# A hybrid decoder layer on one core: where the token sums lie in SBUF, when attention's rows are loaded, and how far ahead gated rows are fetched

## The chip, the cores and the metric

The kernel runs on one core of a Trainium2 chip. The time is that of one execution on the device in microseconds, the median of three runs. The engines are TensorE (PE), VectorE (DVE), ScalarE (ACT), GpSimd (POOL) and SyncE (SP, which issues most DMAs); each runs its own instructions in the order in which they stand, and semaphores join them.

## The reference

One decoder layer on x (1, 512, 2048) in fp32: token mixing by two groups of heads in parallel, then a gated MLP with a short causal convolution.

```python
h = rmsnorm(x, attn_pre_norm)
proj = h @ w_in                       # gq, gk, gv, gg, ga, dq, dk, dv
log_a = log_sigmoid(ga @ w_alpha_up + b_alpha) / 16
o_a = gla_chunked(gq, gk, gv, log_a)  # 4 heads, dk 128, dv 256
o_a = rmsnorm(o_a, gla_norm) * silu(gg)
o_b = diff_attention(dq, dk, dv, lam) # 4 heads: softmax(q1 k1) - lam softmax(q2 k2), causal, ALiBi
o_b = rmsnorm(o_b, diff_norm) * (1 - lambda_init)
x = x + rmsnorm(concat(o_a, o_b) @ w_o, attn_post_norm)
h = rmsnorm(x, ffn_pre_norm)
a, b = split(h @ w_ffn_in)            # 2 x 5632
f = (gelu(causal_conv3(a)) * b) @ w_ffn_out
x = x + rmsnorm(f, ffn_post_norm)
```

## The kernel before

Every fp32 operand is split in two fp32r parts, hi (ScalarE, L125 or L138) and lo (VectorE, L126 or L139), and a product is three products on TensorE. Activations are held whole and transposed in `ah` and `al`. Weights stream in granules of 128x1024 (512 KB) through the tiles `raw` and `rt`, loaded by SP or, with an addition on the way, by POOL, and split into `whi` and `wlo`. A granule of `mm_n` (L182 to L184) is four groups of six 128x512 products.

Most projections run by Strassen's scheme, as a `Unit`: seven segments x0, z0, y0, z1, x1, y1, y2 with sums of activations (s5, s2, s3, s7) and sums of weights. The activation sums, here called token sums, are made once on VectorE by generators in the list `fill`; a call of `step()` draws as much from it as `pace[0]` says, and `drain()` draws the rest. The sums s5, s2 and s3 lie in the pool `so`.

The stages in order of time:

1. `first_half(0)` (0 to about 53 us on VectorE) loads x, normalizes it (L411), transposes it (L146) and multiplies the first four value granules. Its tiles lie in the pool `sa`, closed afterwards. The remaining value granules follow in `proj_n`, whose outputs `gvs` are stored to `gvd`. In between `fill` draws the token sums (`mixer_sums`, rows of `q`) and the forget gate's input (`forget_in`: `gas`, then 32 products, L556 and L557). Then come the eight units. The pool `mb` holds their outputs, the tiles of the setup (masks, `keep`, the lambdas, the columns `cols`), `gas`, `gvs` and the sums s7 (`s7r`); its tag `u` has four slots that all of these share.
2. From about 400 us the attention's steps are woven into the projections of the last head, of the gates (`proj_n` on C_GG) and of `w_o`. `tick()`, called after each group of six products, moves two chains by their paces (`GLA_PACE`, `DIFF_PACE`) and takes one entry from the list `turns`. A GLA head (`gla_head`, `gla_tail`) starts with the scores (L753), then decay rows (L727, L728), seven levels of products (L744) with masks (L747), a state and an output. Its inputs are DRAM rows that the units stored: `gr` (q, k, decay), `dr`, `dv`, `gv`. In `gla_rows(c)` the gated rows of two heads are fetched (`sg` from `sgd`, `ro` from `god`), multiplied (L962), transposed (L146) and split into `ah` and `al`.
3. `w_o`, the norms, and the feed-forward part, which starts with `first_pair(0)` and `first_pair(1)` by `proj_t` and then runs units with sums of its own, `up_sums` (L1198 to L1215).

Inside the manual schedules the order on TensorE is that of the code (in the first half and at the feed-forward start that of all engines); elsewhere a list scheduler sets the order on each engine, from the same code and from the buffers' release. A tile of a pool that lies on another pool's space waits for that space's last reader.

The lines in words that need showing are these two:

```python
gla_in = {0: gla_load(0)}      # after drain() and sums.close()
diff_load(0)
```

and the rows in `gla_rows`: `turns.extend(lambda t=t: run(t) for t in range(NT + 2))`, so that one tick fetches row t and transposes row t − 2.

## Time and profile before

| what | value |
|---|---|
| time, median of 3 runs | 2148.69 us (2147.42 to 2149.38) |
| the profiled execution's own time | 2146.62 us |
| its span | 2144.9 us |
| mean granted TensorE clock | 0.991 |
| PE, DVE, ACT, POOL busy | 97%, 72%, 45%, 12% |
| DMA traffic | 353.30 MB, mean 165 GB/s |

The span is what the profiler records, from the first to the last instruction; the rest of the execution's time lies around it. In rows of the timeline the columns are start, duration, engine, line, operation, output and inputs, how many in a row, and in brackets how long the engine was idle before and what released it. [...]

### The profile page before, as it was taken

Reading aid. Unit: us, or ns where it says so; the run is one execution under the profiler, and the core shown is the slowest. Engines: PE = TensorE matmul, PEld = TensorE weight load, DVE = VectorE, ACT = ScalarE, POOL = GpSimd, SP = SyncE. Lnnn points to the kernel's source line nnn. Section 1 sums busy time; section 2 is a strip of 40 time slices with the busy share of each in tenths; the row PEclk is TensorE's granted clock in tenths of the full one; section 3 lists DMA queues with packets and bytes.
Section 4 is the critical chain, followed back from the end, with each engine's and each line's share of the span. In section 5 each row is a group of like instructions: output and inputs, shape, how many; then the busy total and the mean of one; then the engine's idle time right before and its main releaser. Section 6 shows DMA issues by size and latency. Waiting matters only on the chain.

```text
span 2144.9 us, 34818 instructions
## 1 busy us (share of the span) xinstructions
PE 2081.1 (97%) x14161; PEld 1901.4 (89%) x14161; DVE 1553.2 (72%) x1873; ACT 960.9 (45%) x1217; POOL 260.1 (12%) x297
## 2 busy tenths in 40 slices
PE   7999999899999999989999999999999999999997
PEld 5899999788777888889999999999999887888886
DVE  7967667577764236487878787786777877988987
ACT  5445344344643234245444544554554554544433
POOL 2110111012110000001111111111111011110101
PEclk9999999999999999999999999999999999999999
DMA  7676775744345344346675776757667787676653
GB/s 260 149 178 156 165 178 120 257 139 143 114 137 206 96 138 167 128 99 148 142 190 141 172 173 149 175 140 191 149 161 191 223 215 187 170 196 174 175 159 137
DMA packets 253731, 353.30 MB, mean 165 GB/s; under 512 B 14128, under 2 KB 183524, under 8 KB 251780
## 3 DMA queue, kind: packets, MB, share of 16 engines
q1 hardware_dynamic: 181956, 266.14, 36.5%
q0 software_dynamic: 71616, 84.95, 24.8%
q8 instruction: 111, 1.82, 0.3%
q14 instruction: 48, 0.39, 0.1%
HBM read 303.33 MB, written 47.71 MB: 164 GB/s over the span
## 4 chain that ended last, share of the span: by engine, by line
PE 29%; issue 24%; DVE 3%; POOL 2%; DMA 2%; ACT 0%; POOLq 0%; DVEq 0%; ACTq 0%
PE bank L322 8%; PE bank L321 8%; PE bank L320 8%; PE bank L163 1%; PE bank L161 1%; PE bank L162 1%; DVE wlo L126 1%; POOL rt L234 1%; POOL raw L234 1%; DMA raw<-in_w_ffn_out_dram 1%; PE bank L1430 0%; PE bank L1431 0%; PE bank L1429 0%; DMA raw<-in_w_ffn_in_dram 0%; DVE u L1463 0%
## 5 line engine op out<-in xcount | busy, mean ns | idle before, releaser
L125 ACT ACTIVATE whi<-raw 128x1024 fp32r<-128x1024 f32 x314 | 331.7, 1060 | 554.6 <-PE bank L321 183.7
L126 DVE TENSOR_TENSOR wlo<-raw,whi 128x1024 fp32r<-128x1024 f32 x314 | 381.4, 1220 | 257.9 <-ACT whi L125 257.6
L125 ACT ACTIVATE whi<-rt 128x1024 fp32r<-128x1024 f32 x306 | 322.8, 1060 | 359.2 <-PE bank L321 200.6
L126 DVE TENSOR_TENSOR wlo<-rt,whi 128x1024 fp32r<-128x1024 f32 x306 | 373.2, 1221 | 141.1 <-ACT whi L125 140.5
L320 PE MATMUL bank<-ah,whi 128*128 128x256 f32 x1600 | 443.2, 277 | 3.9 <-ACT gvs L535 2.0
L322 PE MATMUL bank<-ah,wlo 128*128 128x256 f32 x1600 | 443.3, 277 | 2.3 <-DVE wlo L126 2.3
L321 PE MATMUL bank<-al,whi 128*128 128x256 f32 x1600 | 442.8, 277 | 0.0
L320 PEld LDWEIGHTS bank<-ah,whi 128*128 128x128 f32 x1600 | 301.4, 188 | 5.1 <-ACT gvs L535 2.5
L322 PEld LDWEIGHTS bank<-ah,wlo 128*128 128x128 f32 x1600 | 301.3, 188 | 2.9 <-DVE wlo L126 2.8
L321 PEld LDWEIGHTS bank<-al,whi 128*128 128x128 f32 x1600 | 301.2, 188 | 0.1
L1306 PE MATMUL bank<-wlo,ah 128*128 128x512 f32 x560 | 218.2, 390 | 1.3 <-DVE wlo L126 1.3
L1307 PE MATMUL bank<-whi,al 128*128 128x512 f32 x560 | 217.8, 389 | 0.0
L1305 PE MATMUL bank<-whi,ah 128*128 128x512 f32 x560 | 213.1, 390 | 4.5 <-DVE acc L1313 1.8
L182 PE MATMUL bank<-whi,ah 128*128 128x512 f32 x448 | 185.6, 416 | 0.1
L183 PE MATMUL bank<-wlo,ah 128*128 128x512 f32 x448 | 176.6, 395 | 0.4 <-DVE wlo L126 0.2
L184 PE MATMUL bank<-whi,al 128*128 128x512 f32 x448 | 176.4, 395 | 0.0
L1305 PEld LDWEIGHTS bank<-whi,ah 128*128 128x128 f32 x560 | 104.9, 188 | 28.8 <-ACT whi L125 3.9
L1306 PEld LDWEIGHTS bank<-wlo,ah 128*128 128x128 f32 x560 | 105.1, 188 | 23.9 <-DVE wlo L126 2.0
L1307 PEld LDWEIGHTS bank<-whi,al 128*128 128x128 f32 x560 | 105.1, 188 | 21.8
L322 PE MATMUL bank<-s2h,wlo 128*128 128x256 f32 x400 | 111.5, 279 | 1.9 <-DVE wlo L126 1.9
L320 PE MATMUL bank<-s3h,whi 128*128 128x256 f32 x400 | 110.8, 277 | 1.4 <-ACT s3h L138 1.4
L320 PE MATMUL bank<-s5h,whi 128*128 128x256 f32 x400 | 110.6, 277 | 1.0 <-ACT whi L125 1.0
(278 smaller groups left out, 4341.9 us busy)
## 6 DMA issues: line engine op xcount, KB each, us to landing
raw<-in_w_ffn_in_dram SPq DMA_DIRECT2D x96, 512.0 KB, 5.1
raw<-in_w_in_dram SPq DMA_DIRECT2D x64, 512.0 KB, 4.5
raw<-in_w_ffn_out_dram SPq DMA_DIRECT2D x48, 512.0 KB, 5.5
rt<-in_w_ffn_in_dram SPq DMA_DIRECT2D x40, 512.0 KB, 6.3
rt<-in_w_ffn_in_dram POOLq DMA_DIRECT2D x40, 512.0 KB, 5.9
raw<-in_w_ffn_in_dram POOLq DMA_DIRECT2D x40, 512.0 KB, 7.2
raw<-in_w_o_dram SPq DMA_DIRECT2D x32, 512.0 KB, 3.9
rt<-in_w_ffn_out_dram SPq DMA_DIRECT2D x20, 512.0 KB, 6.8
```

The source lines that it names most:

```text
L125: act(hi, raw, AF.Copy)
L126: tt(lo, raw, hi.bitcast(F32), ALU.subtract)
L182: mm(banks[t], ah[:, t, s, :], w[0][:, k, :], start=st, stop=False)
L183: mm(banks[t], ah[:, t, s, :], w[1][:, k, :], start=False, stop=False)
L184: mm(banks[t], al[:, t, s, :], w[0][:, k, :], start=False, stop=sp)
L234: nc.gpsimd.dma_start(out=raws[g].rearrange("p (a b) -> p a b", a=self.a), in_=self.block(0, j, g), accum_op=ALU.add)
L320: mm(o, wh, sh[:, :, kk, :], start=start and kk == 0 and n == 0, stop=False, **NOW)
L321: mm(o, wh, sl[:, :, kk, :], start=False, stop=False, **NOW)
L322: mm(o, wl, sh[:, :, kk, :], start=False, stop=kk == HK - 1, **NOW)
L1305: mm(b[j], sh[:, o:o + P], w[0][:, q, :], start=start and st == 0, stop=False, **NOW)
L1306: mm(b[j], sh[:, o:o + P], w[1][:, q, :], start=False, stop=False, **NOW)
L1307: mm(b[j], sl[:, o:o + P], w[0][:, q, :], start=False, stop=st == 3, **NOW)
```

## The change

It has these parts:

- The pool `so` of the token sums opens at the other end of SBUF (`side="right"`, with a pad tile), in a stack of its own, `early`. The pools `rq` and `mb`, which lay behind it, move down; they now lie on the space of `sa`, the first half's pool.
- `early` closes in the last unit, behind its z1, the last product with a token sum. In its place opens the pool `ga`, which takes the rows of the attention (`gr`, `dr`, `dv`, `gv`, `qb`) and the staging tiles `qs` and `sg`. The loads of the first GLA head and the first differential head are issued there, the other GLA heads' at the third step of the head before (n == 2).
- The unit's loads for x1 get a method of their own, `fetch21`, which the last unit calls ahead of the GLA rows.
- Gated rows: `gla_rows(0)` is called a granule earlier (i == 6), `gla_rows(1)` at i == 1 of `w_o`; a row is fetched at every second tick and so transposed four ticks after its fetch, not two.
- `GLA_PACE` goes from 1.45 to 1.5; the closing loop ends when `turns` is empty too.
- `proj_t` calls `step()` after each granule where it has no tick, which is so in `first_pair(1)` alone.

```diff
-GLA_PACE, DIFF_PACE = 1.45, 0.68
+GLA_PACE, DIFF_PACE = 1.5, 0.68
...
     def proj_t(w3, col, emit, order=tuple(range(KT // 4)), tick=None):
...
+            if tick is None:
+                step()
...
+        def fetch21(self):
+            self.b21 = [load(self.block(1, 0, g), self.a) for g in range(2)]
+
         def x1(self):
-            self.b21 = [load(self.block(1, 0, g), self.a) for g in range(2)]
+            if self.b21 is None:
+                self.fetch21()
...
-    so = sums.enter_context(tc.tile_pool(name="so", bufs=1, reuse_waits="tile"))
+    early = ExitStack()
+    so = early.enter_context(tc.tile_pool(name="so", bufs=1, side="right", reuse_waits="tile"))
     room["rt"] = rq = sums.enter_context(tc.tile_pool(name="rq", bufs=4, reuse_waits="tile"))
     mb = sums.enter_context(tc.tile_pool(name="mb", bufs=2, reuse_waits="tile"))
     up_room(so)
+    so.tile([P, 120], F32, name="pad", bufs=1)
...
         u.y0()
         u.z1()
+        if nxt is None:
+            early.close()
+            ga = mixer.enter_context(tc.tile_pool(name="ga", bufs=2, side="right", reuse_waits="tile"))
+            u.fetch21()
+            gla_in[0] = gla_load(0)
...
         if not u.x_done:
             u.x1()
+        if nxt is None:
+            diff_load(0)
         u.y1()
...
-    gla_in = {0: gla_load(0)}
-    diff_load(0)
-
     def gla_chain():
         for h in range(GH):
-            if h + 1 < GH:
-                gla_in[h + 1] = gla_load(h + 1)
             old = list(tails)
             tails.clear()
-            for _ in gla_head(h, *gla_in[h]):
+            for n, _ in enumerate(gla_head(h, *gla_in[h])):
+                if n == 2 and h + 1 < GH:
+                    gla_in[h + 1] = gla_load(h + 1)
...
-            sg = mc.tile([P, S], F32, name="sg", tag="sg", bufs=3)
+            sg = ga.tile([P, S], F32, name="sg", tag="sg", bufs=3)
             dma(sg, sgd[c][:, t, :])
             o = mc.tile([P, S], F32, name="ro", tag="ro", bufs=2)
...
-        def run(t):
-            if t > 1:
-                transpose_into_act(at[t - 2], t - 2, 8 + 4 * c, 4)
-            if t < NT:
-                fetch(t)
-
-        turns.extend(lambda t=t: run(t) for t in range(NT + 2))
+        def run(i):
+            if i % 2 == 0:
+                t = i // 2
+                if t > 1:
+                    transpose_into_act(at[t - 2], t - 2, 8 + 4 * c, 4)
+                if t < NT:
+                    fetch(t)
+
+        turns.extend(lambda i=i: run(i) for i in range(2 * NT + 3))
...
-        if i == 7:
+        if i == 6:
             gla_rows(0)
 
     def after_out(i):
         if i == 1:
+            gla_rows(1)
             reload(2)
-        if i == 2:
-            gla_rows(1)
...
-        while chains:
+        while chains or turns:
             tick()
```

Three places in the order of instructions follow; the changed kernel's line numbers are higher than the profile's by 2 to 14. The first is VectorE's order at the start of the program in the kernel before: the setup's tiles (`setup`, `keep`, `masks`) come ahead of the first rows of x.

```order
L73 MEMSET nhalf 128x4
L486 MEMSET setup 128x64 x7
L492 MEMSET keep 128x512
L493 MEMSET keep 128x4
L489 CAST masks<-setup 128x256 x7
L411 SCALAR_TENSOR_TENSOR xt<-xt,rs,gb 128x512 x2
L126 TENSOR_TENSOR wlo<-raw,whi 128x1024
```

In the changed kernel the same rows stand on VectorE behind the last row of the first half (`al`, L139), among the sums `q` that follow it.

```order
L139 TENSOR_TENSOR al<-bank,ah 128x512 x2
L494 MEMSET setup 128x64 x7
L500 MEMSET keep 128x512
L620 TENSOR_TENSOR q<-ah 128x1024 x2
L501 MEMSET keep 128x4
L497 CAST masks<-setup 128x256
L621 TENSOR_TENSOR q<-q,al 128x1024
L513 TENSOR_TENSOR setup<-setup 128x256
L497 CAST masks<-setup 128x256 x2
```

They have moved from ahead of the first `xt` to behind the last `al`. The second place is the start of attention. On SP the last weight loads and the first rows stand so before:

```order
L50 DMA dqd_90<-u 128x1024
L50 DMA raw<-in_w_in_dram 128x4x256 x7
L50 DMA gr<-gqd_83 128x512
L50 DMA gr<-gkd_85 128x512
L50 DMA gr<-bd_87 128x512
```

and now, with five of the weight loads behind the rows:

```order
L50 DMA dqd_90<-u 128x1024
L50 DMA raw<-in_w_in_dram 128x4x256 x2
L50 DMA gr<-gqd_83 128x512
L50 DMA gr<-gkd_85 128x512
L50 DMA gr<-bd_87 128x512
```

VectorE at the same place, before: one weight split (`wlo`), then the decay rows `d` and only then the scores `sc`.

```order
L357 TENSOR_TENSOR u<-bank,p_3818 128x2x256
L126 TENSOR_TENSOR wlo<-raw,whi 128x1024
L727 TENSOR_TENSOR d<-gr 128x4x64
L728 TENSOR_TENSOR d<-gr 128x4x64
L727 TENSOR_TENSOR d<-gr 128x8x32
```

And now two weight splits and the scores (L776 is L754 of before) ahead of the decay rows (L749 is L727):

```order
L363 TENSOR_TENSOR u<-bank,p_3819 128x2x256
L126 TENSOR_TENSOR wlo<-raw,whi 128x1024 x2
L776 SCALAR_TENSOR_TENSOR sc<-bank,ident 128x512
L749 TENSOR_TENSOR d<-gr 128x4x64
L750 TENSOR_TENSOR d<-gr 128x4x64
```

The decay rows have moved behind a split and a row that need TensorE. The third place is VectorE at the start of the feed-forward part, before: the four weight splits of `first_pair(1)`'s second half, then all of the sums.

```order
L1169 TENSOR_TENSOR u<-u,bank 128x256
L126 TENSOR_TENSOR wlo<-raw,whi 128x1024 x4
L1198 TENSOR_TENSOR u<-ah 128x1024
L1212 TENSOR_TENSOR u<-ah 128x1024
L1198 TENSOR_TENSOR u<-ah 128x1024
L1212 TENSOR_TENSOR u<-ah 128x1024
L1152 SCALAR_TENSOR_TENSOR u<-bank,cols,u 128x511
```

And now, with the first index's sums among the splits (L1211 is L1198 of before):

```order
L1182 TENSOR_TENSOR u<-u,bank 128x256
L1216 TENSOR_TENSOR u<-u,ah 128x1024
L1217 TENSOR_TENSOR u<-u,al 128x1024
L139 TENSOR_TENSOR s2l<-u,s2h 128x1024
L126 TENSOR_TENSOR wlo<-raw,whi 128x1024
L1220 TENSOR_TENSOR u<-u,ah 128x1024
L126 TENSOR_TENSOR wlo<-raw,whi 128x1024
L1221 TENSOR_TENSOR u<-u,al 128x1024
L139 TENSOR_TENSOR s3l<-u,s3h 128x1024
```

Half of the sums have moved ahead of the last splits of that stage.

## The prediction

> **What bounds the kernel now.** The page comes first: it says which engine fills the span.

> ```profile
> PE 2081.1 (97%) x14161; PEld 1901.4 (89%) x14161; DVE 1553.2 (72%) x1873; ACT 960.9 (45%) x1217; POOL 260.1 (12%) x297
> ```

> TensorE is busy for 2081.1 of 2144.9 us. The change leaves all its matrix products in place, so it can win only the 64 us in which TensorE idles, and what TensorE loses at half clock just after such idle times. Next come the waits of TensorE over the whole trace (line that waited, what it waited for, us, times, longest).

> ```profile
> PE bank L753 <- DMA gr<-gkd: 6.6, 1, 6.6
> PE bank L146 <- DVE ro L962: 6.2, 4, 3.2
> PE bank L827 <- DVE on L863: 2.2, 1, 2.2
> ```

> The wait for the first rows of x, at the very start, is not shown; the diff doesn't touch it. The first two shown are waits that the diff addresses: attention rows, gated rows. The table by stage then shows where VectorE is full or empty and where the granted clock fell.

> ```profile
> core 0: us, PE busy (x) PEld busy (x) DVE busy (x) ACT busy (x) POOL busy (x), PEclk, DMA share, GB/s
> 50.00:75.00 25.00, 25.00 (x117) 18.56 (x116) 23.56 (x24) 12.03 (x16) 5.41 (x4) 1.00 0.91 204
> 75.00:100.00 25.00, 21.97 (x182) 20.81 (x181) 23.12 (x22) 11.42 (x15) 0.00 (x0) 1.00 0.19 59
> ...
> 400.00:425.00 25.00, 18.68 (x91) 16.09 (x91) 13.82 (x39) 8.93 (x15) 0.00 (x0) 0.86 0.84 316
> 625.00:650.00 25.00, 17.78 (x81) 13.47 (x80) 13.61 (x28) 9.23 (x20) 3.98 (x8) 0.93 0.63 198
> 650.00:675.00 25.00, 23.60 (x107) 19.00 (x106) 9.87 (x14) 8.30 (x15) 2.09 (x5) 0.93 0.42 134
> 875.00:900.00 25.00, 25.00 (x131) 21.43 (x130) 8.52 (x10) 6.44 (x8) 0.00 (x0) 1.00 0.40 134
> 925.00:950.00 25.00, 18.32 (x133) 17.22 (x133) 25.00 (x25) 10.65 (x12) 2.55 (x2) 0.87 0.32 61
> 950.00:975.00 25.00, 25.00 (x203) 25.00 (x203) 14.64 (x16) 11.38 (x13) 2.55 (x2) 0.92 0.74 169
> ```

> VectorE is nearly full at 50 to 100 us and quite full at 925 to 950, where TensorE is busy for 18.32 of 25 us only. It is a third full at 875 to 900. Elsewhere in the program the orders of before and after are the same row for row, so five places make the sum.

> **1. The first 125 us: a loss.** In the kernel before, the tiles of the setup lie clear of the first half's tiles, and VectorE does that work while TensorE waits for the first x. In the kernel after, they lie on the space of the first half's tiles, and the order shows them behind the last row of that half, "al" at 51.66.

> ```profile
> 0.91 0.55 DVE L486 MEMSET setup<- 128x64 f32 x7
> 1.52 0.48 DVE L492 MEMSET keep<- 128x512 f32 x1
> 4.85 2.52 DVE L489 CAST masks<-setup 128x256 uint8<-128x256 f32 x7 [2.71 <-POOL setup L488]
> 14.32 0.48 DVE L549 MEMSET wup<- 48x512 f32 x1
> 26.03 0.42 DVE L505 TENSOR_TENSOR setup<-setup 128x256 f32<-128x256 f32 x1
> ...
> 46.30 1.21 DVE L612 TENSOR_TENSOR q<-ah 128x1024 f32<-128x1024 f32 x1
> 51.66 1.29 DVE L139 TENSOR_TENSOR al<-bank,ah 128x512 fp32r<-128x512 f32 x2 [0.61 <-ACT ah L138]
> 57.27 0.41 DVE L139 TENSOR_TENSOR gas<-gar,gas 128x256 fp32r<-128x256 f32 x1
> ...
> 78.14 0.39 PE L320 MATMUL bank<-ah,whi 128*128 128x256 f32 x1 [2.00 <-ACT gvs L535]
> ```

> The rows give 0.55+0.48+2.52+0.48+0.42 = 4.45 us, about 5 with the reduce and the two one-column operations, which I put below 0.42 each. Also moved behind the first half are three early passes over q (L612 and its like), 1.2 us each, which leaves 3.6 us empty ahead of 51.66. So VectorE is close to 9 us behind at 53 us. The table leaves it 25−23.56 and 25−23.12 = 3.3 us of slack up to 100; it stays 6 us late through a stretch in which TensorE follows it closely. I laid the new order out by hand with these durations: the forget gate's input "gas", ready at 57.7 before, comes at 72 to 74. Its 32 products now stand together behind the last product of the values; at 0.23 us each and 2.00 of wait behind them they would start at 78.14−2.00−7.4 = 68.7, so they wait 3 to 5 us; the first sums s7r stand behind the store of the values (they take its place), and x1, y0 follow late. Against this the 2.0 us wait for gvs falls away. SyncE's nine small setup loads now go ahead of the four rt loads; those then issue some 4 us later but land before VectorE comes to them, about 68, so I cost them at nothing; if they land later, each us is a us of TensorE. Sum: −7. Bounds: −3.5 (the 5 us of work less half the slack) and −11 (all 9, and 2 more for a late store). I take the middle, since the stage has both idle VectorE later and a full one at first.

> **2. Start of attention: a small gain.** The attention rows queue on SyncE behind seven weight loads, each of which waits for a buffer, and are issued at 398.36; the product that needs them is due at 406.32−6.58 = 399.74.

> ```profile
> 375.03 23.24 SPq L50 DMA_DIRECT2D raw<-in_w_in_dram  x7
> 398.36 0.60 SPq L50 DMA_DIRECT2D gr<-gqd  x1
> 406.32 2.05 PE L753 MATMUL bank<-gr 128*128 128x128 f32 x8 [6.58 <-DMA gr<-gkd]
> 409.02 0.63 PE L163 MATMUL bank<-ah,wlo 128*128 128x512 f32 x1
> 413.42 0.39 PE L163 MATMUL bank<-ah,wlo 128*128 128x512 f32 x1
> 413.65 1.00 PE L744 MATMUL bank<-qe,d 128*128 128x64 f32 x8
> ...
> 406.98 0.43 DVE L727 TENSOR_TENSOR d<-gr 128x256 f32<-128x256 f32 x1 [9.11 <-DMA gr<-bd]
> 410.28 0.68 DVE L754 SCALAR_TENSOR_TENSOR sc<-bank,ident 128x512 f32<-128x512 f32 x1
> 412.89 1.22 DVE L126 TENSOR_TENSOR wlo<-raw,whi 128x1024 fp32r<-128x1024 f32 x1
> ```

> After the wait, products take 0.63 us instead of 0.39: half clock, for some seven of them, 1.6 us. In the new order the rows are issued behind two weight loads of that row of seven, at about 378 by their places in it, and land well before. The 6.58 us go. But VectorE's new order puts one weight split (L126) and the score row (L754) ahead of the decay rows (L727), and that split waits for a slot that TensorE frees six products after L753, at about 402. ScalarE's and VectorE's parts of the split are 2.3 us, the score 0.68, the eight decays up to 0.43 each, one exponential and two more rows 1.3 beside part of them: L744's input is ready at about 409, while TensorE comes to it, 18 products of 0.23 after L753, at 404.7. That is a new wait of 4 us, likely with half clock again (−1.7). L744 starts at 409 rather than 413.65: +4.7−1.8 = +2.9. Bounds: 0 (the loads collide and the wait is as long) and +8.2 (no new wait, 6.58 and 1.6 of half clock saved).

> **3. Attention, 425 to 625 us: nothing, ±5.** The GLA pace of 1.5 for 1.45 puts each step 3% earlier against the work that feeds it; The largest wait there is L827's 2.2 us for "on". It could go, with as much again of half clock and smaller waits (about +5), or as much could come on top (−5). No row decides; I take 0, the middle.

> **4. Gated rows, 625 to 675 us: a gain.**

> ```profile
> 647.67 1.08 PE L146 MATMUL bank<-ident,ro 128*128 128x128 f32 x4 [3.17 <-DVE ro L962]
> 648.98 0.63 PE L183 MATMUL bank<-wlo,ah 128*128 128x512 f32 x1
> ```

> Before, each transposition follows its fetch by two steps of six products, 1.4 us each, and a load takes longer. After, it follows by four, and the first rows are fetched a granule (5.4 us) earlier. The waits are 6.2 us in four, with about 2 on smaller feeds, and two stretches at clock 0.93: 0.07 × 50 = 3.5 us lost. Together 11.5; of that I leave 2 for the fourth row, whose load still queues on SyncE behind the store of the fourth gate. Gain +9.5, bounds +6 (one wait with its half clock stays) and +11.5.

> [...]

> **5. Start of the feed-forward part, 865 to 960 us: a gain.** `step()` in `proj_t` draws the up sums one piece a granule instead of all at once in `drain()`.

> ```profile
> 885.87 1.23 DVE L126 TENSOR_TENSOR wlo<-raw,whi 128x1024 fp32r<-128x1024 f32 x1 [4.13 <-ACT whi L125]
> 896.75 1.23 DVE L126 TENSOR_TENSOR wlo<-raw,whi 128x1024 fp32r<-128x1024 f32 x1 [4.21 <-ACT whi L125]
> 897.89 1.22 DVE L1198 TENSOR_TENSOR u<-ah 128x1024 f32<-128x1024 f32 x1
> ...
> 937.05 0.58 PE L322 MATMUL bank<-s2h,wlo 128*128 128x256 f32 x1 [1.89 <-DVE wlo L126]
> 945.13 0.38 PE L320 MATMUL bank<-ah,whi 128*128 128x256 f32 x1 [1.03 <-ACT whi L125]
> 947.02 0.58 PE L320 MATMUL bank<-s3h,whi 128*128 128x256 f32 x1 [1.39 <-ACT s3h L138]
> 949.60 0.58 PE L322 MATMUL bank<-ah,wlo 128*128 128x256 f32 x1 [2.00 <-DVE wlo L126]
> ```

> The sums start at 897.89, after VectorE idled 4.2 us three times in a row, and then fill it until TensorE starves: 1.89+1.03+1.39+2.00 = 6.3 us of waits, and clock 0.87 and 0.92, which is 3.3 and 2.0 us. In the new order ten of the long rows (1.14 us from one start to the next) stand in the idle stretch, 11 us of work earlier. I find one wait of under 2 us left by hand. Gain +8 of 11.6; bounds +4 and +11.

> **Sum.** −7 + 2.9 + 0 + 9.5 + 8 = +13.4 us off the profiled execution's 2146.62, so 2133.2. That execution lies 2.1 us under the median of the runs shown, 2148.69; against it the time is 2135.3.

> **Rivals.**
> - No wait takes the place of the one at attention's start (the score row finds its slot free sooner): +8.2 in place of +2.9, so 2130. For it: VectorE idles 9.11 us there. Against it: the order puts L126 ahead.
> - The early sums bring nothing, because TensorE at 925 to 950 waits for weights and not for the sums: 2135.3+8 = 2143. For it: the rows of 937.05 and 949.60 wait on wlo. Against it: those wlo stand behind sums on a full VectorE.
> - Attention gives it all back: the tighter pace makes each of the 28 GLA steps wait; it needs 13 us of 28 steps, 0.45 each. Then the time stays, 2148. Against it: in the trace only one or two steps wait.
> - Slower: the setup chain. The place is the forget gate's products at 69 us: setup loads, masks on POOL, casts, gas, all in a row, TensorE behind. Each us that the chain passes 73 us is a us lost. With a delay of 18 us beyond mine it ends at 2153 or later; from 13 us on nothing is won. For it: nine loads, fourteen selects and the casts now run in one line. Against it: before, casts and selects together ended at 7.4 us.

> **How the numbers follow.** The forecast has 0.60, with its own range 2128 to 2143; the missing wait 0.12; the sums for nothing 0.10; all given back 0.10; slower 0.08. A change under 0.2% (4.3 us) can't be told from none. The first three are faster: 0.82; the fourth the same: 0.10; slower 0.08. The range must leave out no more than 0.2: it runs from 2126 (the gains at their bounds, the setup at its middle) to 2147, which takes in the second and third case and half the fourth.

> **What would show it.** A wait of L753 for gr near zero, and a new one of L744 of about 4 us with half clock behind it; TensorE waiting 3 to 5 us ahead of the gate's products near 70 us; waits for ro under 2 us in all; VectorE over 18 us busy in the 25 us ahead of the sums' old start, and TensorE's waits up to the end of x1 there under 3 us. The prediction is wrong if the first 125 us lose more than 11 us, if attention's middle shifts by over 5, or if the waits for ro only move.

## The result and the profile after

The changed kernel takes 2134.1 us (median of 4 runs, 2132.49 to 2135.74) against 2149.03 us before (4 runs): ratio 0.9934, 95% interval 0.9917 to 0.9951. Forecast were 2135.3 us, 2126 to 2147. The profiled execution has a span of 2130.6 us, 14.3 less than before.

The waits of TensorE over the whole trace of the changed kernel (line that waited, what it waited for, us, times, longest; line numbers are 2 to 22 higher than before, L766 is L744, L328 is L322, L842 is L827):

```profile
PE bank L328 <- DVE wlo L126: 4.8, 6, 2.6
PE bank L766 <- DVE d L759: 4.1, 1, 4.1
PE bank L564 <- DVE gas L139: 2.7, 1, 2.7
PE bank L842 <- DVE on L878: 2.6, 1, 2.6
PE bank L842 <- ACT aT L867: 2.0, 1, 2.0
...
PE bank L146 <- DVE st L827: 0.9, 1, 0.9
...
PE bank L146 <- DVE ro L974: 0.6, 1, 0.6
```

The 6.6 us for gr are gone and the waits for ro have fallen from 6.2 to 0.6 us. Four waits of 2 us or more are new: the first GLA level (L766), the forget gate's products (L564), the 2.6 us of L328 ahead of y0 near 102 us, and the 2.0 us for `aT` (a row of attention) near 635 us. The same stretches as before in the table by stage, in which PEclk is the share of the full clock that TensorE was granted:

```profile
core 0: us, PE busy (x) PEld busy (x) DVE busy (x) ACT busy (x) POOL busy (x), PEclk, DMA share, GB/s
50.00:75.00 25.00, 22.30 (x99) 16.37 (x98) 23.25 (x41) 8.95 (x14) 13.87 (x18) 1.00 0.92 210
75.00:100.00 25.00, 22.58 (x165) 19.51 (x163) 22.47 (x22) 11.27 (x15) 0.00 (x0) 1.00 0.18 42
...
400.00:425.00 25.00, 20.89 (x113) 18.12 (x112) 13.22 (x29) 9.82 (x12) 0.54 (x1) 0.86 0.80 307
...
625.00:650.00 25.00, 22.06 (x105) 17.15 (x104) 14.94 (x29) 13.06 (x29) 5.96 (x13) 1.00 0.61 188
650.00:675.00 25.00, 24.38 (x120) 20.05 (x119) 12.30 (x17) 8.28 (x15) 1.55 (x2) 1.00 0.59 181
...
875.00:900.00 25.00, 25.00 (x118) 20.95 (x117) 19.11 (x19) 10.35 (x11) 0.00 (x0) 1.00 0.32 108
...
925.00:950.00 25.00, 24.99 (x219) 24.79 (x218) 19.81 (x19) 11.49 (x12) 2.58 (x2) 1.00 0.50 116
```

The row of 875 shows VectorE at 19.11 us where it had 8.52, and in that of 925 TensorE now does 219 products in 25 us where it did 133. At 400 the clock is at 0.86 as before: one wait took the place of the other. At 625 and 650 it is full again.

The weight products are the same in number and nearly the same in order in all kernels here, so the k-th of them can be looked up in each trace. The table gives how many us each kernel gains (+) or loses (−) in a stretch against the profiled execution of the kernel before; stretches are named by the times of before.

| | 0 to 150 | 150 to 425 | 425 to 620 | 620 to 680 | 680 to 980 |
|---|---|---|---|---|---|
| changed | −7.9 | +2.4 | −1.6 | +10.1 | +11.9 |
| e11, the same again | −8.1 | +0.1 | −0.6 | +9.8 | +11.8 |
| e1, step alone | −2.0 | −1.1 | +0.1 | +3.0 | +11.6 |
| e2, gated rows alone | −1.9 | −0.2 | +0.3 | +6.1 | +0.4 |
| e3, setup apart | −6.1 | +2.5 | −0.8 | +10.2 | +11.3 |
| e4, setup late | −8.7 | +2.0 | +0.2 | +10.9 | +11.7 |
| e5, apart and values | −4.5 | +1.8 | +0.7 | +9.6 | +11.4 |
| e6, values alone | −5.2 | +2.0 | +0.5 | +11.1 | +11.6 |
| e7, first step early | −8.1 | +0.9 | −0.9 | +10.4 | +12.0 |
| e8, pace 1.45 | −8.4 | +2.4 | +2.2 | +6.6 | +11.8 |
| e9, rows on rt | −7.8 | −1.9 | −0.8 | +10.5 | +11.7 |
| e10, gated undone | −7.7 | +1.7 | +0.3 | +2.7 | +11.6 |
| e12, as e5 | −4.5 | +3.2 | +0.6 | +11.3 | +11.7 |

The sum for the changed kernel is 14.9 up to 980 us; the last 1100 us, where nothing was changed, take back 0.6. How far one execution is to be trusted can be read from the cells in which nothing was changed: e1 differs from the kernel before by −2.0, −1.1, +0.1 and +3.0 ahead of its own edit. So of a single cell only differences over 2 or 3 us count, unless several kernels repeat them. Behind 980 us, where no kernel here changes anything, one execution differs from another by up to 10 us: e4 gains 0.4 there (its span is 2128.4 us) and e7 loses 9.7 (2140.3 us). A whole time therefore tells less of an edit than its own stretch does.

### The profile page after: what moved, and what is told of

The parts are those of the page before. It is cut to its first block, busy times and chain, and to the rows that moved or that the text cites. A ratio compares the mean times of both kernels' runs of the same rounds, so it can differ in the third digit from the quotient of the medians.

```text
span 2130.6 us, 34820 instructions
## 1 busy us (share of the span) xinstructions
PE 2077.2 (97%) x14161; PEld 1898.4 (89%) x14161; DVE 1551.7 (73%) x1873; ACT 961.0 (45%) x1217; POOL 264.2 (12%) x297
## 4 chain that ended last, share of the span: by engine, by line
issue 38%; PE 12%; DVE 3%; POOL 3%; DMA 3%; ACT 0%; POOLq 0%; DVEq 0%; ACTq 0%; SPq 0%
PE bank L326 3%; PE bank L328 3%; PE bank L327 3%; POOL rt L236 2%; POOL raw L236 1%; DVE wlo L126 1%; DMA raw<-in_w_ffn_out_dram 1%; DMA rt<-in_w_ffn_in_dram 1%; PE bank L1319 1%; PE bank L1320 1%; PE bank L1318 1%; DMA rt<-in_w_ffn_out_dram 0%; PE bank L1443 0%; PE bank L1444 0%; PE bank L1442 0%
## 5 line engine op out<-in xcount | busy, mean ns | idle before, releaser
L125 ACT ACTIVATE whi<-raw 128x1024 fp32r<-128x1024 f32 x314 | 331.7, 1060 | 537.0 <-PE bank L327 159.3
L126 DVE TENSOR_TENSOR wlo<-raw,whi 128x1024 fp32r<-128x1024 f32 x314 | 382.2, 1223 | 239.5 <-ACT whi L125 239.1
L125 ACT ACTIVATE whi<-rt 128x1024 fp32r<-128x1024 f32 x306 | 322.7, 1059 | 354.6 <-PE bank L327 180.9
L126 DVE TENSOR_TENSOR wlo<-rt,whi 128x1024 fp32r<-128x1024 f32 x306 | 373.5, 1222 | 139.2 <-ACT whi L125 138.8
L328 PE MATMUL bank<-ah,wlo 128*128 128x256 f32 x1600 | 443.4, 277 | 1.1 <-DVE wlo L126 1.1
L328 PEld LDWEIGHTS bank<-ah,wlo 128*128 128x128 f32 x1600 | 300.4, 188 | 2.1 <-DVE wlo L126 1.9
L328 PE MATMUL bank<-s2h,wlo 128*128 128x256 f32 x400 | 111.3, 278 | 2.7 <-DVE wlo L126 2.6
L328 PE MATMUL bank<-s5h,wlo 128*128 128x256 f32 x400 | 111.0, 278 | 1.1 <-DVE wlo L126 1.1
```

Source lines behind the costliest of these rows:

```text
L125: act(hi, raw, AF.Copy)
L126: tt(lo, raw, hi.bitcast(F32), ALU.subtract)
L328: mm(o, wl, sh[:, :, kk, :], start=False, stop=kk == HK - 1, **NOW)
```

## The experiments

**e1, the step alone.** The kernel before with one edit:

```diff
+            if tick is None:
+                step()
```

> The kernel before with the one call of step() at the end of proj_t's granule and nothing else. Theory: TensorE was starved at 934 to 950 us by sums made all at once, so this line alone gains what the trace of the whole change shows from 930 to 980 us, 11.9 us: about 2137 us, and no wait of TensorE over 1 us between 925 and 960. Rival: the gain there came from the other parts (another phase of the weights' buffers): then under 3 us, 2146 or more.

Measured: 2137.2 us, ratio 0.9951 (0.9934 to 0.9968). The table by stage of e1:

```profile
875.00:900.00 25.00, 25.00 (x132) 21.51 (x132) 18.41 (x20) 10.54 (x11) 0.00 (x0) 1.00 0.39 129
925.00:950.00 25.00, 24.98 (x220) 24.79 (x219) 20.92 (x21) 11.37 (x12) 2.58 (x2) 1.00 0.50 114
```

TensorE has no wait of note at 925 to 970 and the gain of the stretch is 11.6 us, that of the whole change. Two lines that move part of the sums into VectorE's idle time make most of the result.

**e2, the gated rows alone.** The kernel before with the new `run(i)`, i == 6 and i == 1, pace 1.45, all else as it was.

> The kernel before with the gated rows' part alone: fetch at every second tick, begun at i == 6 and i == 1, GLA pace left at 1.45, loads and pools as before. Theory: the waits for ro came from the load standing two ticks ahead of its transposition; this alone gains 8 to 10 us between 620 and 680 us: about 2140 us. Rival: it also needs the rows of GLA to end earlier (pace 1.5 and the earlier start): then the waits for ro move to the call of gla_rows and the gain is under 4 us: 2145 or more.

Measured: 2143.11 us, ratio 0.9975 (0.9964 to 0.9987). The stretch gains 6.1 us, under the theory's 8 and over the rival's 4. TensorE's waits in it are no longer put down to the product of ro and sg but to rows of attention (window 620 to 690 of e2; the last line is VectorE's):

```profile
PE bank L146 <- DVE s L829: 3.4, 1, 3.4
PE bank L800 <- ACT aT L852: 1.2, 1, 1.2
...
631.82 0.69 DVE L962 TENSOR_TENSOR ro<-ro,sg 128x512 f32<-128x512 f32 x1 [5.19 <-DMA sg<-sgd]
```

The row s stands on VectorE behind this product and starts at 633.57. VectorE has idled 5.19 us for the load of sg, so the load of a gated row is still what TensorE waits for, by way of another row.

**e8, the pace.** `GLA_PACE, DIFF_PACE = 1.45, 0.68` in the changed kernel.

> The changed kernel with the GLA pace back at 1.45. If the tighter pace cost the 1.7 us lost between 425 and 620 us, these come back; and if the gated rows need the earlier end of GLA (the gated part alone gained 6.1 us, the whole 10.1), about 4 us are lost between 620 and 680: together 2136 us. If the pace has no part in either: within 1 us of the changed kernel, 2134.

Measured: 2135.69 us, ratio 0.9942 (0.9926 to 0.9957). With 1.45 the middle of attention gains 2.2 us, where ten executions with 1.5 stand between −1.6 and +0.7; the stretch of the gated rows (620 to 680) gains 6.6, much as in e2, where the kernels with 1.5 and the longer distance have 9.6 to 11.3. The same 3.4 us wait as in e2 (there L829, here L844) stands in it:

```profile
PE bank L146 <- DVE s L844: 3.4, 1, 3.4
```

So the pace takes some 2 us in the middle and gives some 4 at the gated rows: worth little by itself. The 2.2 is one execution; sorting the kernels by the clock bears it out. Where a stretch of half clock (3.41 us long in the kernel before, at 554.39, and in the changed kernel, at 561.68) stands near 560 us, 1.45 has 0 to +0.3 (before, e1, e2) and 1.5 has −1.6 to −0.8 (changed, e3, e9); where none does, 1.45 has +2.2 (e8) and 1.5 has −0.9 to +0.7.

**e10, the gated rows undone.** The changed kernel with `run(t)`, i == 7 and i == 2 of before and the pace of 1.5.

> The changed kernel with the gated rows as before (a fetch at every tick, begun at i == 7 and i == 2), the GLA pace left at 1.5. The gated part alone gained 6.1 us between 620 and 680 us, the pace 3.5 on top of it. If the two add up: 3 to 4 us of the 10.1 remain here, about 2140.5. If the pace is of use only with the longer distance: 0 to 1 remain, 2143.5.

Measured: 2142.05 us, ratio 0.9958 (0.9941 to 0.9975). The stretch gains 2.7 us, no more than e1 with the old code (+3.0). Measured from e1, the pace alone gives nothing, the distance alone (e2) 3.1, both together 7.1; so the pace seems to help only together with the longer distance, though the 2.7 us by themselves lie nearer to the first of the two forecasts. The waits for ro are back (window 610 to 690 of e10, and its clock):

```profile
PE bank L146 <- DVE ro L974: 3.5, 3, 2.1
PE bank L146 <- ACT do L886: 2.0, 1, 2.0
...
650.00:675.00 25.00, 23.91 (x109) 19.74 (x107) 9.51 (x14) 7.56 (x13) 0.74 (x2) 0.90 0.50 150
```

**e9, attention's rows on rt's place.** Calls of the loads behind the units, and the pool in another place:

```diff
-            ga = mixer.enter_context(tc.tile_pool(name="ga", bufs=2, side="right", reuse_waits="tile"))
...
+    ga = mixer.enter_context(tc.tile_pool(name="ga", bufs=2, reuse_waits="tile"))
     mc = mixer.enter_context(tc.tile_pool(name="mc", bufs=2, reuse_waits="tile"))
```

> The changed kernel with the pool of the attention's rows opened on the left after the units are done, on the space of rt and u, and not in the token sums' place; the loads are called behind the units, as before. SyncE's order then has the rows behind seven weight loads again and VectorE's the decay rows ahead of the second split. Theory: the start of attention is that of the kernel before: a wait for gr of 5 to 7 us, no wait of 4 us at the first level; 2 to 3 us lost against the changed kernel by 416 us, about 2136.5. Rival: the loads were not the point, the 4 us come from the chain score, decay, level: then both waits stand and 5 us or more are lost, 2139.

Measured: 2136.53 us, ratio 0.9935 (0.9913 to 0.9957), not told from the changed kernel by its time. In the trace the stretch loses 1.9 where the changed kernel gains 2.4 (and 0.1 in e11). The wait of before is back and the new one is gone (window 375 to 430):

```profile
PE bank L772 <- DMA gr<-gkd: 8.1, 1, 8.1
```

In the order of instructions (no run has this), moving the calls alone leaves SyncE's rows where the changed kernel has them; only with the other place do the seven weight loads stand ahead of them again. Which space the pool lies on sets when the rows load.

**e7, the first step early.**

```diff
     with tc.manual_schedule(engines={ET.PE}):
+        advance("gla")
         for h in range(STRASSEN_HEADS, DH):
```

> The changed kernel with the first step of the GLA chain (scores and first decays) called once ahead of the last head's projection instead of at its third tick; the rest of the chain so comes one step earlier. Theory: the new wait of 4.1 us at L766 exists because one weight split that waits for TensorE stands ahead of the decay rows; with the rows ahead of it the wait falls under 1.5 us and its half clock goes, 4 to 6 us gained by 430 us, about 2129 us. Rival: the 4 us are the length of the chain from score to decay to product, which only moves along: then a wait of 3 to 4 us stays, 2133.

Measured: 2139.02 us, ratio 0.995 (0.993 to 0.9969). Neither theory holds. VectorE did come to the decay rows 6 us earlier, and then stood again:

```profile
406.53 0.42 DVE L749 TENSOR_TENSOR d<-gr 128x256 f32<-128x256 f32 x1
...
412.55 0.42 DVE L758 SCALAR_TENSOR_TENSOR qe<-d,gr 128x256 f32<-128x256 f32 x1 [2.65 <-DMA dkd<-u]
...
413.45 1.94 PE L766 MATMUL bank<-qe,d 128*128 128x64 f32 x8 [5.58 <-DVE d L759]
```

The first row of the next step, qe, waits for the store of a unit's output u into dkd: its pool `mc` lies on u's space. That store bounds the first level at 413 us however early the rows are. It would have been next had the 4.1 us been removed. The kernel's time, 4.9 us above the changed kernel's, is not made here: the stretch is 1.5 us behind, and in its trace most of the rest lies behind 980 us.

**e3, the setup apart.** The setup's two tiles in a pool of their own, closed before the sums' pool opens:

```diff
+    apart = ExitStack()
+    sp0 = apart.enter_context(tc.tile_pool(name="sp0", bufs=2, side="right", reuse_waits="tile"))
+    sets = [sp0.tile([P, GR], F32, name="setup", tag="setup") for _ in range(2)]
...
+    apart.close()
     sums = ExitStack()
```

> The changed kernel with the two setup tiles in a small pool of their own at the right end of SBUF, closed before the token sums' pool opens there, so that the setup can run during the first half again. Theory: the 8.0 us lost by 120 us all come from the setup standing behind the first half; most of it returns, 6 to 9 us: about 2127 us. Rival: it comes from the rest of the tiles that moved onto the first half's space (rt, gar, wup, the sums' q): then at most 2 us, 2132 or more.

Measured: 2131.49 us, ratio 0.9922 (0.9908 to 0.9937). In the trace only 1.9 us of the first stretch come back: the theory fell, the rival's bound of 2 holds. ScalarE and VectorE in e3 show what is left:

```profile
76.76 1.21 ACT L546 ACTIVATE gvs<-bank 128x256 f32<-128x256 f32 x4 [6.39 <-DMA gvd<-gvs]
77.83 2.03 ACT L138 ACTIVATE s2h<-q 128x1024 fp32r<-128x1024 f32 x2
...
78.94 1.22 DVE L139 TENSOR_TENSOR s2l<-q,s2h 128x1024 fp32r<-128x1024 f32 x1 [5.12 <-ACT s2h L138]
...
101.25 0.38 PE L328 MATMUL bank<-s2h,wlo 128*128 128x256 f32 x1 [3.71 <-DVE wlo L126]
```

ScalarE waits until the first tile of the values is stored, since the second takes its slot; both s2h splits stand behind it, and VectorE waits for them. In the kernel before the wait was 3.54 us and the first s2h stood ahead of it, because the sums q had begun during the first half.

**e4, the setup late, the slots free.** e3 with this line for each of the two tiles:

```diff
+        nc.vector.tensor_copy(v.rearrange("p (a b) -> p a b", b=64)[:, :, 0], al[:, NT - 1, KT - 1, 0:16].bitcast(F32))
```

> As e3, but each of the two setup tiles is first written with 16 numbers of the first half's last result, so that the setup's work comes behind the first half again, while the four slots of u stay free of it (gas does not stand behind the columns, s7r not behind the store of the values). Theory A, VectorE is full there and the work itself costs: most of the loss is back, 4 to 7 us over e3, about 2132. Theory B, it is the slots (gas behind the columns, s7r behind the store): within 2 us of e3, about 2128.

Measured: 2132.24 us, ratio 0.993 (0.9914 to 0.9946), not told from e3 by its time. The first stretch loses 8.7 against 6.1 us in e3: 2.6 us by the trace, between the two theories' numbers. Of these, 1.4 are waits of TensorE for the setup's own loads (L518 and L520), which neither e3 nor the changed kernel has, so e4 doesn't decide between the work and the slots.

**e5, apart and values.** e3 with the second tile of the values in the two p1 slots:

```diff
+            gvs.append(pair_tile("gvs").rearrange("p n (t e) -> p (n t) e", e=256))
+            gvs.extend(mb.tile([P, 2, 256], F32, name="gvp", tag="p1", bufs=2) for _ in range(2))
```

> e3 with the second tile of the staged values put into the two p1 slots instead of a slot of u (its store becomes two). In e3 ScalarE stood 6.39 us on the store of the first tile, whose slot the second one takes, and the splits s2h behind it came late. Theory: that wait is what e3 still loses by 120 us; without it TensorE's wait before y0 (3.71 us) and its half clock go, 4 to 6 us gained over e3, about 2126 us. Rival: VectorE is late anyway, because the token sums q now start behind the first half: then s2l comes no earlier than 76 us, under 2 us gained, 2130 or more.

Measured: 2131.71 us, ratio 0.9919 (0.9901 to 0.9937). ScalarE's wait is gone and s2l starts 1.3 us earlier, at 77.67 (78.94 in e3):

```profile
76.53 1.22 DVE L602 TENSOR_TENSOR s7r<-ah 128x1024 f32<-128x1024 f32 x1 [2.52 <-DMA gvd<-gvs]
77.67 1.22 DVE L139 TENSOR_TENSOR s2l<-q,s2h 128x1024 fp32r<-128x1024 f32 x1
...
98.83 0.58 PE L328 MATMUL bank<-s2h,wlo 128*128 128x256 f32 x1 [3.50 <-DVE wlo L126]
```

But s7r stands on the store in its turn, and the wait before y0 stays at 3.5 us. 1.6 us come back, the rival's "under 2". What is left, 4.5 against the 0 to 2.0 that kernels with the old layout show, I put down to the sums q, which begin behind the first half; that is not shown, since no kernel moves them alone.

**e6, the values alone,** on the changed kernel.

> The changed kernel with only that edit on the staged values, the setup left behind the first half. If the wait on the store is the larger part of the 8 us lost: 3 to 5 us gained, about 2130 us. If VectorE's late work is: under 2 us, 2132 or more, and TensorE's waits for wlo before y0 stay near 3 us.

Measured: 2132.23 us, ratio 0.9924 (0.9906 to 0.9941). 2.7 us of the first stretch come back, between the two; the wait before y0 is 3.5 us. It and e3 add up in part: 2.7 and 1.9 alone, 3.4 together.

**e11 and e12, the changed kernel and e5 side by side.**

> The changed kernel again, for a comparison with e12 in the same runs: 2134, within 1.5 us.

> e5 again, setup apart and the values' second tile in p1, beside the changed kernel. By the trace of e5 it gains 3.5 us in the first 150 us and nothing elsewhere: 2131, 2 to 4 us under e11. Rival: the two gains of the first 125 us are taken back by TensorE's wait before y0, which stayed at 3.5 us: within 1 us of e11.

Measured: 2136.21 us (ratio 0.993, 0.9913 to 0.9947) and 2132.4 us (0.9918, 0.99 to 0.9935), 6 runs each. The medians differ by 3.8 us and the traces by 3.6 in the first stretch; the intervals overlap, so by the times alone it isn't sure that e5 is better. e11 came out 2.2 us above its forecast, outside the 1.5. e5 loses the least in the first stretch, but by their times e3, e4, e5 and e6 can't be told apart.

## Why the prediction was right

**The sum** was 13.4 us, and 14.3 were measured between the profiled spans (14.9 between the medians); four of five terms lie within their bounds, the fifth 0.9 above. That the sum is right to 1 us is in part luck: the terms miss by −0.9, −0.5, −1.6, +0.6 and +3.9, and 0.6 are lost behind 980 us. The second profiled execution (e11) gains 8.8, since some 4 us are lost there.

**1. First 125 us, −7: measured −7.9, for a reason that was half wrong.** The gate's products waited 2.70 us, just under the forecast of 3 to 5; gas was ready at 71.6, just ahead of the 72 to 74. But I put nearly all of it on the setup's late work, and e3 gives that 1.9 us, e4 against e3 2.6, of which 1.4 have another cause. I had overlooked a queue that the change doesn't name: ScalarE's wait for the store of the values grew from 3.54 to 5.49 us, and what now stands behind it are the sums. My working had VectorE 9 us behind and let it catch up 3.3; the number came out, as far as the runs tell, because store and sums together cost what I had given to the setup, which is luck. The setup loads did not push the rt loads back, either: SyncE had issued them by 51, and rt went out at 51.05, not 4 us later than before (52.61).

**2. Start of attention, +2.9: measured +2.4,** +0.1 in e11. The new wait was forecast as 4 us and is 4.11, with the clock at 0.86 behind it:

```profile
410.91 1.23 DVE L126 TENSOR_TENSOR wlo<-raw,whi 128x1024 fp32r<-128x1024 f32 x1 [5.04 <-ACT whi L125]
412.05 0.68 DVE L776 SCALAR_TENSOR_TENSOR sc<-bank,ident 128x512 f32<-128x512 f32 x1
412.65 0.42 DVE L749 TENSOR_TENSOR d<-gr 128x256 f32<-128x256 f32 x1
...
416.84 1.94 PE L766 MATMUL bank<-qe,d 128*128 128x64 f32 x8 [4.11 <-DVE d L759]
```

VectorE idles 5.04 us for a split that TensorE holds up, with the decay rows behind it, though their inputs were issued at 386 and took 5.5 to 6.8 us. The chain from there to L766 is the one laid out. The rival without a new wait is out, and e7 shows that its price, +8.2, wasn't to be had in full: the store of u comes next.

**3. Middle of attention, 0 ± 5: measured −1.6,** −0.6 in e11. The size is what e8 gives to the pace, 1 to 2 us. The working had no row for it and took the middle.

**4. Gated rows, +9.5: measured +10.1.** The waits for ro fell as laid out, and the one that stayed is 0.6 us. The 2 left for a late load came back larger and under other names (VectorE and ScalarE of the changed kernel):

```profile
635.87 0.69 DVE L974 TENSOR_TENSOR ro<-ro,sg 128x512 f32<-128x512 f32 x1 [5.07 <-DMA sg<-sgd]
...
633.31 0.60 ACT L958 ACTIVATE sg<-bank 128x512 f32<-128x512 f32 x1 [2.24 <-DMA sgd<-sg]
```

Behind the first stands the row st, for which TensorE waits 0.9 us, behind the second the row aT, for which it waits 2.0. The size is also in part the execution's: with the old code of this stage e1 waited 2.7 us for ro where the kernel before waited 6.2, and gained 3.0 in the stretch. Measured from e1 the step is worth 7.1, still within its bounds. What it left out is that neither part makes it alone: the pace without the distance brings nothing.

**5. Feed-forward start, +8: measured +11.9, above the bound of 11.** The mis-sized term is the wait that I left: I found one of under 2 us by hand and set the bounds so, and the trace has none. The whole of 11.6 was there to be had, and e1 shows that the line alone brings it. The rival that the sums bring nothing is out.

The forecast of no change by a tighter pace, and the slower one by the setup chain, are out as well: the gate's products waited 2.7 us, not 18 more.

## What to carry to other kernels

Work that an engine can do in idle time and has queued for a full stretch is worth looking for first: here two lines that moved ten rows of VectorE into idle time some 30 to 54 us earlier brought three quarters (by the times) to four fifths (by the traces) of the gain of a change of many parts. A pool's place is a decision on time: what was once on free space begins to wait when it is put on space in use (the setup's rows start at 52.11 us instead of 0.91), and its loads go out earlier when that space is free earlier (the first gr at 386.23 us instead of 398.36). When a wait is removed, follow the engine's next rows with their buffers; here a split, and behind it a store, stood ready to take its place.

## What the runs showed of the hardware

The clock did not follow the length of a wait. In the kernel before, weight products behind a wait of 2.16 us take 0.63 us instead of the 0.39 to 0.40 to which they return (TensorE's rows from 553):

```profile
553.60 0.88 PE L827 MATMUL bank<-dr 128*128 128x384 f32 x2 [2.16 <-DVE on L863]
...
555.53 0.63 PE L182 MATMUL bank<-whi,ah 128*128 128x512 f32 x1
...
557.97 0.39 PE L182 MATMUL bank<-whi,ah 128*128 128x512 f32 x1
```

In the changed kernel a wait of 2.63 us does the same, while the stage from 100 us, with the wait of 2.59 us before L328 in it, keeps its full clock, as do those of 50 and 75 us shown above with the wait of 2.70 (its rows of the timeline, and of the table by stage):

```profile
560.38 1.62 PE L842 MATMUL bank<-dr 128*128 128x384 f32 x4 [2.63 <-DVE on L878]
...
562.65 0.63 PE L186 MATMUL bank<-whi,al 128*128 128x512 f32 x1
```

```profile
100.00:125.00 25.00, 21.68 (x179) 21.21 (x180) 19.72 (x20) 10.27 (x10) 2.55 (x2) 1.00 0.51 137
550.00:575.00 25.00, 22.37 (x111) 18.70 (x111) 17.14 (x44) 15.75 (x29) 3.07 (x7) 0.93 0.29 87
```

```profile
66.75:70.16 3.41, 2.27 (x10) 1.53 (x9) 3.30 (x7) 2.45 (x6) 1.28 (x1) 1.00 1.16 230
70.16:73.58 3.42, 1.87 (x9) 1.02 (x10) 3.42 (x5) 0.06 (x1) 1.27 (x1) 1.00 1.21 234
73.58:76.99 3.41, 3.41 (x16) 1.83 (x15) 3.41 (x4) 1.28 (x5) 0.00 (x0) 1.00 1.16 274
...
558.27:561.68 3.41, 1.30 (x5) 0.86 (x5) 2.32 (x7) 1.90 (x5) 0.14 (x1) 1.00 0.86 214
561.68:565.09 3.41, 3.41 (x9) 2.65 (x8) 2.28 (x7) 1.40 (x2) 0.00 (x0) 0.50 0.16 59
```

Here a half-clock window took some 1.7 us of work (an estimate: half of 3.41), and of the waits of 2 to 3 us in these two traces some were followed by one and some were not. This is what two executions show; no run shows what sets the marks. The ten executions of the changed kernel (e11 among them) have mean granted clocks of 0.993 to 0.996, so the same program is not granted the same clock each time. The rows of PEclk follow the products closely: in the kernel before the products at 0.63 us start at 554.68 to 557.24 us, the window at half clock spans 554.39 to 557.80, and the product at 557.97 is back at 0.39.

Executions of one program differ by more than their repeated cells would suggest: the changed kernel's two spans are 2130.6 and 2136.1 us (e11), and 3.6 of these 5.5 us arise behind 980 us in code that no kernel here changes. Why they differ there is open.
